# A decoder trunk on one core: the whole kernel in written order, native float32 scores of two heads in row halves, heads and accumulators in pairs

## The chip, the cores and the metric

The kernel runs on one core of a Trainium2 chip. The metric is the device time of the program in microseconds (us), as the median of three runs. PE is the tensor engine (TensorE), PEld its weight loads, DVE the vector engine, ACT the scalar engine, POOL the GpSimd engine and SP the sync engine, which here only issues DMAs. L12 is line 12 of the kernel.

## What is computed

One layer of a decoder for 256 tokens of 2048 values, in float32, with rms norms. `a` is the normed input:

```
in  = a @ W_in                      # 2048 x 2368: q and kv latents, rope key, window q, k, v
mla = 8 heads: softmax(causal((q_nope k_nope + q_rope k_rope) / sqrt(192))) v     # 256 x 256 each
swa = 16 heads of 64, 2 kv heads: softmax over the last 128 keys with a T5 bias and a sink
x  += [mla, swa] @ W_out            # 2048 x 2048
x  += relu(rms(x) @ W_up)**2 @ W_down   # 2048 x 8192, 8192 x 2048
out = rms(x)
```

The T5 bias of a head is a table of 32 values, looked up by a bucket of the distance of query and key (16 exact distances, then 16 logarithmic steps).

## The kernel before, in words

Every wide product is transposed: weights are the 128x128 stationary tile, the activation is the moving one, with 256 tokens as columns. Each weight block of 1024 columns is loaded by SP, rounded to a high part by ACT (L104, 1050 ns) and a low part by DVE (L105, 1253 ns); the activation holds a high and a low part as 512 columns. `mm_chunk` multiplies the high weight with all 512 columns (L114) and the low weight with the 256 high ones (L116). I call these two products **a pair**; 1024 weight columns are 8 pairs, and I call that **a step**. There are 64 pairs of the first four output tiles (k, v and two q tiles, L264 and L268), 240 of the other 15 tiles of the projection `in`, 32 of `kn`, a product for `v`, 48 of `qb`, 256 of `wo` and 2016 of `up` and `dn`, and the last two output tiles of `dn` in row halves (L764).

What stands between the pairs on PE:

- the T5 bias: sixteen tiles of 512 one-hot columns. Each is multiplied with the table's high and low part (L302, L303, 64 output rows), copied by ACT (L304) and written to DRAM by POOL's queue (L307); four loads bring it back in another layout (L314), and POOL masks the first half (L317).
- the window heads, two at a time (`t` = 0 to 7): scores `sa` and `sb` (L392, L396) of q and k split into high and low parts; DVE adds the bias (L403 to L407), maxima, ACT exponentials (L422) and the scaling by 1/sum (L428); four transposes (L435); the product with `v_sc`, which is padded with zeros so that two heads add up in one tile of 128 rows (L444, L448).
- the MLA heads, one at a time beside the first half of `wo`: `mla_scores` (L625 to L630), three transposes, `mla_pv`.
- the final norm: sums (L794), 32 transposes of the result (L804), a scaling of each group of four and a DMA of it, eight in all.

The order on each engine is set by the framework's scheduler from priorities and its own estimates, not by the order in which the code is written. PSUM is held in tiles of 512 columns: four for accumulators (`psd`), two for scores (`pss`), two for the rest (`pst`).

## Time and profile before

| what | us |
|---|---|
| median of three runs (lowest, highest) | 1032.0 (1028.16, 1032.9) |
| the profiled execution | 1032.6 |
| its span, first to last instruction | 1030.8 |
| PE busy | 1008.3 |
| DVE busy | 705.0 |
| ACT busy | 539.5 |

A row of a timeline gives the start, the length, the engine, the line, the operation, and output <- inputs with the shape. The length of a product is longer than the distance to the next one, since products are pipelined, so the distance of starts is what a product costs. A row marked x4 stands for four instructions; a native float32 product is recorded as two.

### The profile page before, as it was taken

Reading aid. Unit: us, or ns where it says so; the run is one execution under the profiler, and the core shown is the slowest. Engines: PE = TensorE matmul, PEld = TensorE weight load, DVE = VectorE, ACT = ScalarE, POOL = GpSimd, SP = SyncE. Lnnn points to the kernel's source line nnn. Section 1 sums busy time; section 2 is a strip of 40 time slices with the busy share of each in tenths; the row PEclk is TensorE's granted clock in tenths of the full one; section 3 lists DMA queues with packets and bytes.
Section 4 is the critical chain, followed back from the end, with each engine's and each line's share of the span. In section 5 each row is a group of like instructions: output and inputs, shape, how many; then the busy total and the mean of one; then the engine's idle time right before and its main releaser. Section 6 shows DMA issues by size and latency. Waiting matters only on the chain.

```text
span 1030.8 us, 15494 instructions
## 1 busy us (share of the span) xinstructions
PE 1008.3 (98%) x5854; PEld 886.8 (86%) x5854; DVE 705.0 (68%) x1123; ACT 539.5 (52%) x893; POOL 105.7 (10%) x112
## 2 busy tenths in 40 slices
PE   9989789999999999999999999999999999999997
PEld 8878678889888888888888888888888888888887
DVE  7895589798897866655566656566666556666664
ACT  6675599965664444333444433344443334445553
POOL 2121340551232200000000000000000000000000
PEclk9999899999999999999999999999999999999999
DMA  8957523353454655555555555555555555555552
GB/s 299 317 206 210 155 91 141 135 188 129 161 185 164 216 192 185 193 193 187 187 195 191 185 192 195 184 189 198 186 185 195 192 185 191 196 185 187 194 172 82
DMA packets 53450, 191.04 MB, mean 185 GB/s; under 512 B 6096, under 2 KB 6480, under 8 KB 52864
## 3 DMA queue, kind: packets, MB, share of 16 engines
q1 hardware_dynamic: 51840, 184.57, 51.1%
q0 software_dynamic: 1392, 5.41, 2.2%
q8 instruction: 46, 0.75, 0.3%
q14 instruction: 28, 0.23, 0.1%
q10 hardware_dynamic: 144, 0.07, 0.0%
HBM read 185.80 MB, written 4.23 MB: 184 GB/s over the span
## 4 chain that ended last, share of the span: by engine, by line
PE 85%; DMA 4%; DVE 4%; ACT 4%; issue 2%; POOL 0%; ACTq 0%; POOLq 0%; DVEq 0%
PE up L114 23%; PE dn L114 22%; PE up L116 12%; PE dn L116 11%; PE wo L114 5%; PE wo L116 3%; DMA raw_in<-in_w_in_dram 2%; DMA bias<-bias_scratch 2%; PE in L114 2%; DVE lo_in L105 1%; PE in L116 1%; PE dn L764 1%; PE yp L444 1%; ACT st L422 0%; DVE buck L243 0%
## 5 line engine op out<-in xcount | busy, mean ns | idle before, releaser
L114 PE MATMUL up<-ms,hi_up 128*128 128x512 f32 x1024 | 355.4, 392 | 0.0
L116 PE MATMUL up<-ms,lo_up 128*128 128x256 f32 x1024 | 287.7, 281 | 0.0
L104 ACT CAST hi_dn<-raw_dn 128x1024 fp32r<-128x1024 f32 x128 | 134.3, 1049 | 201.6 <-PE dn L114 161.2
L105 DVE TENSOR_TENSOR lo_up<-raw_up,hi_up 128x1024 fp32r<-128x1024 f32 x128 | 161.1, 1259 | 114.0 <-ACT hi_up L104 113.6
L114 PEld LDWEIGHTS up<-ms,hi_up 128*128 128x128 f32 x1024 | 192.1, 188 | 42.1
L104 ACT CAST hi_up<-raw_up 128x1024 fp32r<-128x1024 f32 x128 | 134.2, 1049 | 174.3 <-issue 133.6
L105 DVE TENSOR_TENSOR lo_dn<-raw_dn,hi_dn 128x1024 fp32r<-128x1024 f32 x128 | 156.9, 1226 | 96.1 <-ACT hi_dn L104 91.0
L116 PEld LDWEIGHTS up<-ms,lo_up 128*128 128x128 f32 x1024 | 192.5, 188 | 0.0
L114 PE MATMUL dn<-usB,hi_dn 128*128 128x512 f32 x496 | 174.9, 392 | 0.0
L114 PE MATMUL dn<-usC,hi_dn 128*128 128x512 f32 x496 | 174.9, 392 | 0.0
L116 PE MATMUL dn<-usB,lo_dn 128*128 128x256 f32 x496 | 139.4, 281 | 0.0
L116 PE MATMUL dn<-usC,lo_dn 128*128 128x256 f32 x496 | 139.4, 281 | 0.0
L114 PEld LDWEIGHTS dn<-usB,hi_dn 128*128 128x128 f32 x496 | 93.1, 188 | 20.4
L114 PEld LDWEIGHTS dn<-usC,hi_dn 128*128 128x128 f32 x496 | 93.1, 188 | 20.4
L116 PEld LDWEIGHTS dn<-usB,lo_dn 128*128 128x128 f32 x496 | 93.2, 188 | 0.0
L116 PEld LDWEIGHTS dn<-usC,lo_dn 128*128 128x128 f32 x496 | 93.2, 188 | 0.0
L114 PE MATMUL wo<-ys,hi_wo 128*128 128x512 f32 x256 | 90.5, 395 | 0.2 <-DVE mla L323 0.2
L114 PE MATMUL in<-xs,hi_in 128*128 128x512 f32 x240 | 86.9, 400 | 0.0
L116 PE MATMUL wo<-ys,lo_wo 128*128 128x256 f32 x256 | 72.4, 284 | 0.0
L116 PE MATMUL in<-xs,lo_in 128*128 128x256 f32 x240 | 68.8, 287 | 0.7 <-DVE lo_in L105 0.7
L105 DVE TENSOR_TENSOR lo_in<-raw_in,hi_in 128x1024 fp32r<-128x1024 f32 (+1 forms) x39 | 47.7, 1224 | 17.4 <-ACT hi_in L104 17.2
L114 PEld LDWEIGHTS wo<-ys,hi_wo 128*128 128x128 f32 x256 | 48.0, 188 | 10.4 <-DVE mla L323 0.5
(298 smaller groups left out, 1261.3 us busy)
## 6 DMA issues: line engine op xcount, KB each, us to landing
raw_up<-in_w_up_dram SPq DMA_DIRECT2D x128, 512.0 KB, 3.6
raw_dn<-in_w_down_dram SPq DMA_DIRECT2D x128, 512.0 KB, 3.6
raw_in<-in_w_in_dram SPq DMA_DIRECT2D x37, 512.0 KB, 6.0
raw_wo<-in_w_out_dram SPq DMA_DIRECT2D x32, 512.0 KB, 4.2
raw_qb<-in_w_q_b_dram SPq DMA_DIRECT2D x6, 512.0 KB, 3.7
xt<-in_x_tok_dram SPq DMA_DIRECT2D x2, 1024.0 KB, 8.1
bias_scratch<-biasT POOLq DMA_DIRECT2D x4, 512.0 KB, 5.3
bias<-bias_scratch POOLq DMA_DIRECT2D x4, 512.0 KB, 9.9
```

The source lines that it names most:

```text
L104: nc.scalar.copy(hi[:, :n], raw[:, :n])
L105: nc.vector.tensor_tensor(lo[:, :n], raw[:, :n], hi.bitcast(F32)[:, :n], op=ALU.subtract)
L114: nc.tensor.matmul(ps[:, 0:2 * S], lhsT=hi[:, col:col + P], rhs=act(k, 0, 2 * S), start=first, stop=False)
L116: nc.tensor.matmul(ps[:, S:2 * S], lhsT=lo[:, col:col + P], rhs=act(k, 0, S), start=False, stop=last)
L444: nc.tensor.matmul(yp[:, 0:S], lhsT=v_sc[:, 0, t // 4, j, :], rhs=pt[:, j, 0:2, :].rearrange("p i c -> p (i c)"), start=(j == 0), stop=False)
L764: nc.tensor.matmul(ps[:, b * S:(b + 1) * S].rearrange("p (a c) -> p a c", a=2), lhsT=hi[:, (k % 8) * P:(k % 8 + 1) * P], rhs=x[:, :, b, :] ...
```

## The change

The code is laid out as 332 steps of 8 pairs in a loop under `manual_schedule`, in which each engine keeps the order in which the code is written. Tables `pre`, `hook` and `post` name what is issued ahead of a step, before its k-th pair, and behind it; `w_hi` of a step is issued three steps ahead, `w_lo` two. The projection `in` takes steps 0 to 29, `kn` 30 to 33, `v` 34 to 37, `qb` 38 to 43, `wo` 44 to 75, then `up` and `dn`. Further:

- window scores: native float32 products of the unsplit q and k of 64 rows, one head in rows 0 to 63 and the other in rows 64 to 127 of the array (`swa_mm`: two products of 128 columns and two of 256); pair t at step 17+3t, its transposes at step 20+3t, its v product at 21+3t, where the two heads take the two column halves of the array instead of zero-padded values.
- T5 bias: the one-hot columns come from the distances themselves (ACT takes the absolute difference to an interval's middle, DVE compares), so the bucket loop on DVE is gone; four batches of four native float32 products of 512 columns, again in column halves; each batch is written to DRAM and loaded again by itself, and the mask comes at the end.
- MLA heads in pairs (`mla_mm`): native float32, 128 rows for the part without rope, row halves for the rope part.
- accumulators in pairs of 512 columns (`psd` two pairs, `pss` one), read by one instruction for two tiles.
- the roots for x, kv and q from a bit estimate and three Newton rounds on DVE instead of ACT's Sqrt; rope's turn by DMAs on POOL's queue; squares are added on DVE instead of POOL.
- the tail: 24 of the 32 final transposes, unscaled, stand in the last quarter of `dn` (`fin_turn`), four more ahead of the last row half; the result goes out in six DMAs on two queues.

PE, the projection, where the first bias tile stands. Before, `oh` is a one-hot tile, `rel_hi` and `rel_lo` the table, `in4` an output tile of the projection:

```order
L302 MATMUL bias0_0_679<-oh0_0_677,rel_hi_370 64x512
L303 MATMUL bias0_0_679<-oh0_0_677,rel_lo_371 64x512
L114 MATMUL in4_676<-xs_77,hi_in4_0_665 128x512
L116 MATMUL in4_676<-xs_77,lo_in4_0_666 128x256
...
L302 MATMUL bias0_1_693<-oh0_1_691,rel_hi_370 64x512
```

After, `g_sb` holds the table in float32, and `in1` is a pair of output tiles:

```order
L723 MATMUL in1_529<-xs_77,hi_6_488 128x512
L725 MATMUL in1_529<-xs_77,lo_6_527 128x256
L322 MATMUL bias0_561<-oh0_509,g_sb_78 64x512
L322 MATMUL bias0_561<-oh1_546,g_sb_78 64x512
L322 MATMUL bias0_561<-oh0_509,g_sb_78 64x512
L322 MATMUL bias0_561<-oh1_546,g_sb_78 64x512
L723 MATMUL in1_529<-xs_77,hi_6_488 128x512
```

Sixteen places with two products became four places with four, and they moved from the projection's fifth to eighth of the 15 tiles to steps 6 to 12, its fourth to seventh.

PE, the first window heads. Before, the scores stand between tiles 9 and 10 of the projection, and the transposes `tp0` of their softmax `st0` two tiles later:

```order
L116 MATMUL in9_1056<-xs_77,lo_in9_1_1052 128x256
L392 MATMUL sa0_1101<-kk_393,qs0_1096 128x256 x2
L396 MATMUL sb0_1102<-kk_393,qs0_1096 128x256 x4
L114 MATMUL in10_1144<-xs_77,hi_in10_0_1133 128x512
...
L114 MATMUL in12_1373<-xs_77,hi_in12_0_1362 128x512
L435 MATMUL tp0_1272<-ident_101,st0_1109 128x128 x2
L116 MATMUL in12_1373<-xs_77,lo_in12_0_1363 128x256
```

After, around the second pair of heads, `sw1` being its scores and `hi_20`, `lo_20` the weights of step 20:

```order
L723 MATMUL in5_1046<-xs_77,hi_20_943 128x512
L725 MATMUL in5_1046<-xs_77,lo_20_988 128x256
L417 MATMUL sw1_1049<-kd_371,q_s0_402 128x128 x2
L417 MATMUL sw1_1049<-kd_371,q_s0_402 128x256 x2
L723 MATMUL in5_1046<-xs_77,hi_20_943 128x512
...
L466 MATMUL tp0_1058<-ident_101,st0_972 128x128 x4
```

The transposes of one pair of heads now stand in the same step as the scores of the next, three steps behind their own scores.

DVE, the softmax of the first window heads. Before, `lo_in12_1` is the low part of a weight block, `bias` the loaded table:

```order
L403 TENSOR_TENSOR st0_1109<-sa0_1101,bias_392 128x2x128
L105 TENSOR_TENSOR lo_in12_0_1363<-raw_in12_0_1361,hi_in12_0_1362 128x1024
L404 TENSOR_TENSOR st0_1109<-sa0_1101,st0_1109 128x2x128
L403 TENSOR_TENSOR st1_1197<-sa1_1189,bias_392 128x2x128
L404 TENSOR_TENSOR st1_1197<-sa1_1189,st1_1197 128x2x128
L105 TENSOR_TENSOR lo_in12_1_1369<-raw_in12_1_1367,hi_in12_1_1368 128x1024
...
L407 TENSOR_TENSOR st0_1109<-st0_1109,bias_392 128x2x128
L407 TENSOR_TENSOR st1_1197<-st1_1197,bias_392 128x2x128
```

After:

```order
L1140 TENSOR_TENSOR lo_19_946<-raw_19_919,hi_19_920 128x1024
L426 COPY_PREDICATED st0_972<-mask_own_106,sw0_950 128x2x128
L429 SCALAR_TENSOR_TENSOR st0_972<-sw0_950,rx8_373,bias_369 128x2x128
L431 SCALAR_TENSOR_TENSOR st0_972<-st0_972,rx8_373,bias_369 128x2x128
L434 TENSOR_REDUCE nm0_977<-st0_972 128x4
L438 TENSOR_TENSOR nm0_977<-nm0_977,nsink_119 128x4
L440 TENSOR_TENSOR es0_980<-nm0_977,nsink_119 128x4
L1140 TENSOR_TENSOR lo_20_988<-raw_20_942,hi_20_943 128x1024
L1140 TENSOR_TENSOR lo_21_1016<-raw_21_984,hi_21_985 128x1024
L457 TENSOR_TENSOR l0_1006<-l0_1006,es0_980 128x4
```

Before, the softmaxes of two pairs of heads are interleaved with the weights of tile 12; after, each stands whole between the weights of steps 19 and 20, and the weights of steps 20 and 21 stand behind the instructions that read the bias.

The diff, cut to its core:

```diff
-    psd = ctx.enter_context(tc.tile_pool(name="psd", bufs=4, space=bass.MemoryType.PSUM))
-    pss = ctx.enter_context(tc.tile_pool(name="pss", bufs=2, space=bass.MemoryType.PSUM))
+    psd = ctx.enter_context(tc.tile_pool(name="psd", bufs=2, space=bass.MemoryType.PSUM))
+    pss = ctx.enter_context(tc.tile_pool(name="pss", bufs=1, space=bass.MemoryType.PSUM))
     pst = ctx.enter_context(tc.tile_pool(name="pst", bufs=2, space=bass.MemoryType.PSUM))
 
...
+    def dense_pair(name):
+        return psd.tile([P, 2, 512], F32, tag="d", name=name)
+
     def dense_ps(name):
-        return psd.tile([P, 512], F32, tag="d", name=name)
+        if not dense_half:
+            t = dense_pair(name)
+            dense_half.append(t[:, 1, :])
+            return t[:, 0, :]
+        return dense_half.pop()
 
     def score_ps(name):
-        return pss.tile([P, 512], F32, tag="s", name=name)
+        return pss.tile([P, 2, 512], F32, tag="s", name=name)
...
+    def newton(y, v, name, n, rounds):
+        t = small(f"nt_{name}", n)
+        for _ in range(rounds):
+            nc.vector.tensor_tensor(t, y, y, op=ALU.mult)
+            nc.vector.scalar_tensor_tensor(t, t, -0.5, v, op0=ALU.mult, op1=ALU.mult)
+            nc.vector.scalar_tensor_tensor(y, t, 1.5, y, op0=ALU.add, op1=ALU.mult)
+        return y
+
+    def rsqrt_bits(v, name):
+        y = small(f"y_{name}")
+        nc.vector.tensor_scalar(y.bitcast(I32), v.bitcast(I32), -0.5, 1597463007.0, op0=ALU.mult,
+                                op1=ALU.add)
+        return newton(y, v, name, 2, 3)
+
...
-    def bias_step(n):
-        b, e = divmod(n, 4)
-        o = b * 2048 + e * 512
-        oh = rot([P, 512], F32R, f"oh{b}_{e}")
-        nc.vector.tensor_scalar(oh, lanes[o // 4096][:, o % 4096:o % 4096 + 512],
-                                c_sb[:, 0:1], None, op0=ALU.is_equal)
-        ps = score_ps(f"bias{b}_{e}")
-        nc.tensor.matmul(ps[0:64, :], lhsT=rel_hi, rhs=oh, start=True, stop=False)
-        nc.tensor.matmul(ps[0:64, :], lhsT=rel_lo, rhs=oh, start=False, stop=True)
-        nc.scalar.copy(bias_box[0][:, b % 2, e * 4:e * 4 + 4, :],
-                       ps[0:64, :].rearrange("p (q c) -> p q c", c=P))
...
+    def oh_away(n):
+        oh = work.tile([P, 2, 512], F32, tag="oh", name=f"oh{n}", bufs=2)
+        o = n * 1024
+        nc.scalar.activation(oh.rearrange("p e c -> p (e c)"),
+                             lanes[o // 4096][:, o % 4096:o % 4096 + 1024], AF.Abs,
+                             bias=c_sb[:, 4:5])
+        oh_state[n] = oh
+
+    def oh_hot(n):
+        oh = oh_state[n]
+        nc.vector.tensor_scalar(oh, oh, c_sb[:, 5:6], None, op0=ALU.is_lt)
+
+    def bias_mm(n):
+        b, par = divmod(n, 2)
+        if par == 0:
+            bias_ps[b] = score_ps(f"bias{b}")
+            return
+        ps = bias_ps[b]
+        ohs = oh_state.pop(n - 1), oh_state.pop(n)
+        for e in range(2):
+            for p2, oh in enumerate(ohs):
+                nc.tensor.matmul(ps[p2 * 64:(p2 + 1) * 64, e, :], lhsT=rel_f, rhs=oh[:, e, :],
+                                 start=True, stop=True)
+
+    def bias_out(b):
+        nc.scalar.copy(biasT[:, b % 2, :, :], bias_ps.pop(b))
+        for p2 in range(2):
+            q0 = b * 16 + p2 * 8
             nc.gpsimd.dma_start(
-                scratch2[:, :, b * 16:(b + 1) * 16, :].rearrange("g h q c -> (g h) q c"),
-                bias_box[0][:, b % 2, :, :])
-
-    def bias_load():
-        for i in range(2):
-            for qh in range(2):
-                nc.gpsimd.dma_start(bias[qh * 64:(qh + 1) * 64, i, :, :],
-                                    scratch2[2 * i + qh].rearrange("h q c -> q h c"))
-            if i == 0:
-                nc.gpsimd.affine_select(out=bias[:, 0, :, :], in_=bias[:, 0, :, :],
-                                        pattern=[[0, NH_SWA], [-1, P]], compare_op=ALU.is_ge,
-                                        fill=NEG, base=0, channel_multiplier=1)
-
-    def sum_evac(dst, ps, name):
-        t = evac_sum(ps, name)
-        nc.vector.tensor_tensor(dst, ps[:, 0:S], t, op=ALU.add)
-
-    def scaled_evac(dst, ps, rstd, name):
-        t = evac_sum(ps, name)
-        nc.vector.tensor_tensor(t, ps[:, 0:S], t, op=ALU.add)
-        nc.vector.tensor_tensor(dst, t, rstd, op=ALU.mult)
+                scratch2[:, :, q0:q0 + 8, :].rearrange("g h q c -> (g h) q c"),
+                biasT[p2 * 64:(p2 + 1) * 64, b % 2, :, :].rearrange("p e (q c) -> p (e q) c", c=P))
+        for g in range(4):
+            q0 = (g % 2) * 64 + b * 16
+            nc.gpsimd.dma_start(bias[q0:q0 + 16, g // 2, :, :],
+                                scratch2[g, :, b * 16:(b + 1) * 16, :].rearrange("h q c -> q h c"))
+
+    def bias_mask():
+        nc.gpsimd.affine_select(out=bias[:, 0, :, :], in_=bias[:, 0, :, :],
+                                pattern=[[0, NH_SWA], [-1, P]], compare_op=ALU.is_ge,
+                                fill=NEG, base=0, channel_multiplier=1)
+
+    def pair_evac(dst, ps, name):
+        t = two(f"t_{name}", "evt2", 2)
+        nc.scalar.copy(t, ps[:, :, S:2 * S])
+        nc.vector.tensor_tensor(dst, ps[:, :, 0:S], t, op=ALU.add)
...
-        a = score_ps(f"sa{t}")
-        b = score_ps(f"sb{t}")
-        for j in range(2):
-            nc.tensor.matmul(a[:, j * S:(j + 1) * S].rearrange("p (w c) -> p w c", w=2),
-                             lhsT=qs[:, j, 0:P], rhs=kk[:, kv, :, 0:P], start=True, stop=True)
-        for j in range(2):
-            for w in range(2):
-                nc.tensor.matmul(b[:, j * S:(j + 1) * S], lhsT=qs[:, j, P:2 * P],
-                                 rhs=kk[:, kv, w, :], start=(w == 0), stop=(w == 1))
...
+    def swa_mm(t):
+        sc = score_ps(f"sw{t}")
+        for qs, cs, w in ((slice(0, P), slice(0, P), P), (slice(P, S), slice(P, P + S), S)):
+            for j, rows in enumerate((lo_h, hi_h)):
+                nc.tensor.matmul(sc[:, j, cs], lhsT=q_sb[t][rows, qs], rhs=kd[rows, t // 4, 0:w],
+                                 start=True, stop=True)
+        box[f"sc{t}"] = sc
+
+    def swa_max(t):
+        sc = box.pop(f"sc{t}")
         st = rot([P, 2, 2, P], F32, f"st{t}")
-        av = a.rearrange("p (j w c) -> p j w c", j=2, w=2)
-        bv = b.rearrange("p (j w c) -> p j w c", j=2, w=2)
         hs = slice(2 * t, 2 * t + 2)
-        nc.scalar.copy(st[:, :, 1, :], bv[:, :, 0, :])
-        nc.vector.tensor_tensor(st[:, :, 0, :], av[:, :, 1, :], bias[:, 0, hs, :], op=ALU.add)
-        nc.vector.tensor_tensor(st[:, :, 0, :], av[:, :, 0, :], st[:, :, 0, :], op=ALU.add)
+        nc.scalar.copy(st[:, :, 1, :], sc[:, :, P:2 * P])
...
+    def swa_pv(t):
+        pt, own = box.pop(f"pt{t}")
         yp = misc_ps(f"yp{t}")
+        kv = slice((t // 4) * 64, (t // 4) * 64 + 64)
         for j in range(2):
-            nc.tensor.matmul(yp[:, 0:S], lhsT=v_sc[:, 0, t // 4, j, :],
-                             rhs=pt[:, j, 0:2, :].rearrange("p i c -> p (i c)"),
-                             start=(j == 0), stop=False)
+            nc.tensor.matmul(yp[j * 64:(j + 1) * 64, 0:S], lhsT=vv[:, 0, kv],
+                             rhs=pt[:, j, :, :].rearrange("p i c -> p (i c)"),
+                             start=True, stop=False)
         for j in range(2):
-            nc.tensor.matmul(yp[:, P:S], lhsT=v_sc[:, 1, t // 4, j, :], rhs=pt[:, j, 2, :],
...
+    def turn_copy(key, src):
+        t = two(f"rt_{key}", "oh", 2)
+        n = src.shape[1]
         for o in range(0, P, 32):
-            nc.scalar.copy(t[o:o + 32, :], src[o ^ 32:(o ^ 32) + 32, :])
...
+    def mla_mm(p):
+        mla = box["mla"]
+        sc = score_ps(f"ms{p}")
+        for qs, cs, w in ((slice(0, P), slice(0, P), P), (slice(P, S), slice(P, P + S), S)):
+            for e in range(2):
+                nc.tensor.matmul(sc[:, e, cs], lhsT=mla[:, QN + 2 * p + e, qs],
+                                 rhs=mla[:, KN + 2 * p + e, 0:w], start=True, stop=False)
+            for e, rows in enumerate((lo_h, hi_h)):
+                nc.tensor.matmul(sc[:, e, cs], lhsT=mla[rows, QR + p, qs], rhs=krr[rows, 0:w],
+                                 start=False, stop=True)
+        box[f"ms{p}"] = sc
...
+    def fin_turn(g):
+        tp = score_ps(f"fo{g}")
+        for b in range(2):
+            for i in range(4):
+                nc.tensor.transpose(tp[:, b, i * P:(i + 1) * P], box["fin"][:, 0, b, 4 * g + i, :],
+                                    ident)
+        box[f"fo{g}"] = tp
+
+    def fin_copy(g):
+        tp = box.pop(f"fo{g}")
...
-            finish(b, g)
+        b = SW0 + 3 * t
+        pe(b, 1, swa_mm, t)
+        at(post, b, swa_max, t)
+        at(post, b + 1, swa_exp, t)
+        at(post, b + 2, swa_norm, t)
+        pe(b + 3, 3, swa_turn, t)
+        at(post, b + 3, swa_pt, t)
+        pe(b + 4, 5, swa_pv, t)
+        at(post, b + 4, y_out, NH_MLA + t)
...
+    def w_hi(n):
+        raw = wpool.tile([P, WH], F32, tag="raw", name=f"raw_{n}")
+        hi = wpool.tile([P, WH + 64], F32R, tag="whi", name=f"hi_{n}")[:, WOFF:WOFF + WH]
+        nc.sync.dma_start(raw, srcs[n])
+        nc.scalar.copy(hi, raw)
+        weights[n] = raw, hi
+
+    def w_lo(n):
+        raw, hi = weights[n]
+        lo = wpool.tile([P, WH + 64], F32R, tag="wlo", name=f"lo_{n}")[:, WOFF:WOFF + WH]
+        nc.vector.tensor_tensor(lo, raw, hi.bitcast(F32), op=ALU.subtract)
+        weights[n] = hi, lo
+
+    with tc.manual_schedule():
+        for n in range(3):
+            w_hi(n)
+        for n in range(2):
+            w_lo(n)
+        for s_ in range(NS):
+            for f in pre.get(s_, ()):
+                f()
+            if s_ + 3 < NS:
+                w_hi(s_ + 3)
+            if s_ + 2 < NS:
+                w_lo(s_ + 2)
+            if s_ < NS:
+                mms[s_](s_, weights.pop(s_))
...
```

## Rows read from the trace of the kernel before

**Rows 1.** The page: busy time; TensorE's granted clock in 40 slices.

```profile
PE 1008.3 (98%) x5854; PEld 886.8 (86%) x5854; DVE 705.0 (68%) x1123; ACT 539.5 (52%) x893; POOL 105.7 (10%) x112
PEclk9999899999999999999999999999999999999999
```

**Rows 2.** Timeline of PE (start us, length us, line, operation), middle of up.

```profile
500.11 0.39 PE L114 MATMUL up<-ms,hi_up 128*128 128x512 f32 x1
...
503.93 0.39 PE L114 MATMUL up<-ms,hi_up 128*128 128x512 f32 x1
```

**Rows 3.** Waits of PE, whole span: us in total, times, longest us.

```profile
PE tp L435 <- ACT st L428: 4.4, 1, 4.4
PE yp L444 <- DVE pt L440: 3.1, 4, 1.4
PE sb L396 <- DVE st L404: 2.4, 1, 2.4
PE vps L365 <- DVE vT L350: 1.5, 1, 1.5
```

**Rows 4.** Timeline of PE, 112 to 130 us: the first window heads.

```profile
113.01 0.40 PE L392 MATMUL sa<-kk,qs 128*128 128x256 f32 x2
...
113.72 0.40 PE L114 MATMUL in<-xs,hi_in 128*128 128x512 f32 x1
...
120.90 0.77 PE L435 MATMUL tp<-ident,st 128*128 128x128 f32 x2 [4.35 <-ACT st L428]
...
123.39 0.63 PE L114 MATMUL in<-xs,hi_in 128*128 128x512 f32 x1
...
126.59 0.40 PE L114 MATMUL in<-xs,hi_in 128*128 128x512 f32 x1
...
127.18 1.02 PE L444 MATMUL yp<-pt,v_sc 128*128 128x256 f32 x4
128.04 0.61 PE L448 MATMUL yp<-pt,v_sc 128*128 128x128 f32 x4
128.49 0.50 PE L195 MATMUL ts_kv<-ones,acc_kv 128*128 128x1 f32 x4
```

**Rows 5.** Timeline of PE, one bias tile and the pair behind it.

```profile
55.05 0.39 PE L302 MATMUL bias<-oh,rel_hi 128*64 128x512 f32 x1
55.28 0.39 PE L303 MATMUL bias<-oh,rel_lo 128*64 128x512 f32 x1
55.51 0.39 PE L114 MATMUL in<-xs,hi_in 128*128 128x512 f32 x1
```

**Rows 6.** Timeline of PE: `wo` begins; the scores of one MLA head.

```profile
202.11 0.50 PE L114 MATMUL wo<-ys,hi_wo 128*128 128x512 f32 x1 [0.18 <-DVE mla L323]
...
205.00 0.28 PE L625 MATMUL ms<-qk 128*128 128x256 f32 x1
...
205.95 0.40 PE L114 MATMUL wo<-ys,hi_wo 128*128 128x512 f32 x1
```

**Rows 7.** Timeline of POOL: the last bias write, the mask behind the loads.

```profile
86.48 0.54 POOL L307 DMA_DIRECT2D bias_scratch<-biasT  x1 [6.88 <-ACT biasT L304]
...
102.86 2.01 POOL L317 TENSOR_SCALAR_AFFINE_SELECT bias<-bias 128x2048 f32<-128x2048 f32 x1 [7.85 <-DMA bias<-bias_scratch]
```

**Rows 8.** DVE, groups by line and form (busy us, mean ns): weights' low parts.

```profile
L105 DVE TENSOR_TENSOR lo_in<-raw_in,hi_in 128x1024 fp32r<-128x1024 f32 x37 | 46.4, 1253 | 16.5 <-ACT hi_in L104 16.3
```

**Rows 9.** Timeline of DVE, two instructions one behind the other.

```profile
124.06 0.42 DVE L328 TENSOR_TENSOR c_q<-t_q,rstd_x 128x256 f32<-128x256 f32 x1
124.39 0.42 DVE L440 TENSOR_TENSOR pt<-tp,mask_ownT 128x256 f32<-128x256 f32 x1
```

**Rows 10.** Timeline of PE and ACT, the tail.

```profile
1019.07 1.11 PE L764 MATMUL dn<-usC,hi_dn 128*128 128x256 f32 x8
...
1020.38 1.29 PE L804 MATMUL fo<-ident,fin 128*128 128x128 f32 x10
...
1024.60 0.69 ACT L809 ACTIVATE fin<-fo,y_f 128x512 f32<-128x512 f32 x1 [0.17 <-PE fo L804]
```

More of the change, by code (lines that the diff above doesn't have):

```diff
@@ L352 @@
[L352 to L362 removed]
+    rx8 = small("rx8")
@@ L378 @@
[L378 to L397 removed]
+        box["vps"] = vps
@@ new lines, in c_add, with c_sums, c_mean @@
+    def c_add(which):
+        a, b = acc_c[which, 0], acc_c[which, 1]
+        nc.vector.tensor_tensor(a, a, b, op=ALU.add)
+    def c_sums(which):
+        ps = misc_ps(f"ts_{which}")
+        a = acc_c[which, 0]
+        for b in range(2):
+            for i in range(2):
+                nc.tensor.matmul(ps[:, b:b + 1], lhsT=a[:, i, b * P:(b + 1) * P],
+                                 rhs=ones[:, 0:1], start=(i == 0), stop=(i == 1))
+        box[f"ts_{which}"] = ps
+    def c_mean(which):
+        v = small(f"ms_{which}")
+        nc.vector.scalar_tensor_tensor(v, box.pop(f"ts_{which}")[:, 0:2], 1.0 / LORA, epsx,
+                                       op0=ALU.mult, op1=ALU.add)
+        box[f"v_{which}"] = v
```

1056 lines of the change are left out of this document (627 added, 429 removed).

## The prediction

> **What bounds the kernel now.** I read the page first. PE is busy for 1008.3 us of the span, 98% [rows 1], so only two things can move the time: what stands on PE, and the few microseconds in which PE waits. In the middle of `up` eleven pairs start within 3.82 us [rows 2], .347 us for a pair and 2.78 for a step of eight. The number of pairs isn't changed, so from `wo` on, where PE runs at this pace, the change can win nothing but can lose. The list of PE's waits shows where it stands still: 4.4 us at the first window transposes, 3.1 at the window value products, 2.4 for a score buffer, 1.5 for the transposes of v, 11.4 in all [rows 3], all ahead of `wo`, which starts at 202.11 [rows 6]. The timeline then shows what such a wait leaves behind: after the 4.35 us stop at 120.90 a wide product lasts .63 instead of .40, and the pace of .40 is back at 126.59 [rows 4]; in the page's row of granted clocks the fifth slice is the only low one of the stretch [rows 1]. Between these times stand seven pairs and four transposes, 7 x .347 + 4 x .113 = 2.9 us at full pace, done in 5.7: 2.8 lost. Last, the length of a product is .39 and the distance to the next start .23 [rows 5]; the difference, .16, comes into the open once after every stop. PE stopped seven times in those four rows: 1.1.
>
> **What goes.** The transposes of a pair of heads stand three steps (8.3 us) behind its scores, with nothing of another pair's softmax ahead of them; before, two softmaxes were interleaved, and the last scaling came 4.4 us too late. The value products stand a step behind the transposes, the score buffer is asked for again after three steps, the transposes of v come long after v. If DVE and ACT keep up, all four waits go, with their restarts and the slow clock: 11.4 + 1.1 + 2.8 = 15.3 us. The waits not shown stay in the sum as an allowance for small new ones.
>
> Whether DVE keeps up: in steps 17 to 42 it has 26 weight blocks of 1.25 us [rows 8], 33 us, eight softmaxes of about ten instructions, 35, and some seventy instructions of evacuations and norms, about .4 each as in [rows 9], 28. That is 96 beside some 92 us of PE work. But an instruction of .42 us is followed by the next after .33 [rows 9], which makes it about 76. I take no wait from this, and keep 4 us (96 - 92) as the upper bound.
>
> **What is put in other forms.** Native float32 costs, from 127.18 to 128.49: two products of 256 columns .86, two of 128 columns .45, so .43 and .225 each, in two records each [rows 4]. Now, for each group, (1) what it costs before; (2) if the two halves of the array run one after the other; (3) if the second record of one half runs beside the first of the other half, since PE takes its instructions in order and neighbours alone can share; (4) if halves run fully side by side.
>
> Bias: before 16 x .46 (55.05 to 55.51, [rows 5]) = 7.4. After, four batches of four products of 512 columns, .86 each: (2) 13.8, (3) five records of .43 instead of eight, 8.6, (4) 6.9.
> Window scores: before 8 x .71 (113.01 to 113.72, [rows 4]) = 5.7. After, two products of .225 and two of .43: (2) 8 x 1.31 = 10.5, (3) 8 x .87 = 7.0, (4) 5.2.
> Window values: before 8 x 1.31 = 10.5; after (2) 10.5, (3) 7.0, (4) 5.2.
> MLA scores: before 8 x .95 (205.00 to 205.95, [rows 6]) = 7.6. After, a pair of heads has 1.31 of full-height products and 1.31 in halves: (2) 10.5, (3) 9.2, (4) 7.9.
> Together against before: (2) +14.1, (3) +.8, (4) -6.0. No row shows two halves of the array at work, so the price lies between (2) and (4). I take (3), which asks only that two neighbours on different rows or columns don't wait for each other. Eight more products of one column (`c_sums`; two took .50 at most, [rows 4]) add up to 2; I take 1.
>
> The Trainium skill ("TensorE: Matmul & The Clock Gate", Part 3 on packing small matmuls) says that products at different tile positions run concurrently in the array; no row here shows it, and by it the sum would come to price (3) or (4).
>
> **The tail.** 28 of the 32 last transposes now stand ahead of the last product instead of behind it. Ten take 1.29 us, less the open .16 .113 each [rows 10]: +3.2 on PE before the last product ends. Behind it, before, the last product ends at 1020.18, the last scaling at 1025.29, and the span at 1030.8. After, there are still two additions, a square, sums, the root, a scaling of 768 columns and one of 512, and DMAs. The root hides no longer behind transposes, but the scaling waited for the last transposes, not for the root, by .17 [rows 10]. I take no change, bounds -1 and +1.5.
>
> **What is hidden.** The bucket loop, the split of q and k, the additions on POOL and the bit-estimate roots are work beside PE. The bit roots add six short DVE instructions each and take an ACT step away; two or more steps lie between the sums and the product that spreads the root, so I cost them at nothing; without that cover each would cost some 1 us. The rope turn goes to POOL's queue, which has nothing queued behind it there.
>
> **The sum.** -15.3 + .8 + 1.0 + 3.2 = -10.3. The profiled execution took 1032.6, .6 over the median of 1032.0; from the median I come to 1021.7, and say 1021.5. The case's own range goes from 1012 (price (4), and the small waits gone too) to 1026 (DVE's 4 us).
>
> **Rivals.**
> *Halves one after the other.* Price (2): 13.3 more, 1035. For it: nothing in the trace runs side by side on PE. Against it: nothing in it could. The change would then be lost in what it pays on PE.
>
> *The bias comes late.* DVE's L429 reads the masked bias in step 17, and `lo_20` and `lo_21` are queued behind it on DVE. Before, 18.4 us passed from the issue of the last write (86.48) to the end of the mask (104.87), 7.85 of it waiting for loads [rows 7]. After, the last batch is copied at the start of step 13, and DVE comes to L429 about 12 us later. If the way takes 18.4 again, DVE stands for 6.4; PE, two steps (5.6) ahead less 3.8 of softmax and weight work, stops for 4.6, and pays a slow clock again, 2.8: 1029. Against it: only a quarter of the table is still under way then, so I'd put the mask 0 to 6 us early.
>
> *Drains, the slower side.* PE now goes from full tiles to half tiles and back: 16 times for window scores, 16 for values, 8 for the bias, 16 for MLA, 56 in all. If PE must empty at each, the open .16 [rows 5] is paid 56 times, +9. With price (2) that is 1044, slower; with price (3) 1030.5. From price (2), .04 us a switch are enough for slower. Against it: the bias tiles of before are 64 columns wide and stand among full ones, and 55.05, 55.28 and 55.51 lie .23 apart, with no gap on the way out of the narrow tile [rows 5]. Row halves have no such row, and a weight load that can't be hidden would make a switch dearer still.
>
> The Trainium skill ("TensorEngine Tiling (Array Packing)", Key Properties) states that changing the tiling mode drains TensorE, which speaks against this change; the row at 55.51 shows no drain for narrow tiles, and no run shows row halves.
>
> **Chances.** Halves shared, bias in time (1021.5): .54. Bias late (1029): .13, of which I give .04 to a lateness so small that the result is still faster. One after the other (1035): .12. Drains with shared halves (1030.5): .07. Drains with halves one after the other (1044): .14. What a measurement of this kernel can tell from no change is about 0.5%, 5.2 us: faster below 1026.8, slower above 1037.2. So faster .54 + .04 = .58, same .09 + .12 + .07 = .28, slower .14. The range from 1011 to 1036 holds all but the last case and about .04 at the ends of the first.
>
> **What would show it.** In the profile after: `wo` starts at about 187 if all is right (202.1 less 15.3; bias +1.2, scores +1.3, values -3.5 and the sums +1.0 cancel), at about 199 with price (2). From the first score product of a pair of window heads to the next wide one .87 says price (3), 1.31 price (2), .66 price (4); for a batch of bias 2.15, 3.44, 1.72. A start more than .23 behind that of the last half tile says drain. The list of waits has no row of over 1 us in the projection, and the slices of the granted clock show no 8 in the fifth; a wait of `lo_20` for L429, and of that for POOL's mask, says late bias. From the end of the last row-half product to the end of the span it is 10.6 (1030.8 less 1020.18, [rows 10]) as before. I'm wrong if PE waits in steps 17 to 42 as often as before, in smaller pieces, for low parts of weights: then DVE is the bound there, or if the steps of `up` are longer than 2.78.

## The result and the profile after

The changed kernel takes 1036.7 us (median of nine runs, 1035.0 to 1040.0) against 1030.8 of the kernel before in the same measurement (nine runs, 1028.2 to 1032.9): ratio 1.0059, 95% interval 1.0043 to 1.0076. It is slower by .6%; I had forecast 1021.5 and faster.

PE's waits of the changed kernel (us in total, times, longest) stand beside those of [rows 3]:

```profile
PE in L725 <- DVE lo L1140: 6.5, 1, 6.5
PE tp L466 <- DVE st L460: 1.8, 2, 1.4
PE in_kv L272 <- ACT hi_in L113: 1.5, 1, 1.5
PE bc_x L370 <- DVE dg_x L364: 1.4, 1, 1.4
PE ts_q L517 <- DVE sq_q L510: 1.2, 1, 1.2
```

Of the four waits of [rows 3] three are gone, as forecast, and the window transposes wait 1.8 in place of 4.4. But one of 6.5 stands in their place. It can be followed upward, from PE's timeline to DVE's and POOL's. First PE, columns as in [rows 4]:

```profile
98.80 0.40 PE L723 MATMUL in<-xs,hi 128*128 128x512 f32 x1
105.67 0.58 PE L725 MATMUL in<-xs,lo 128*128 128x256 f32 x1 [6.48 <-DVE lo L1140]
...
111.35 0.63 PE L723 MATMUL in<-xs,hi 128*128 128x512 f32 x1
```

PE has the high part of step 20's weights, but not the low part. DVE, which makes it:

```profile
91.23 0.45 DVE L426 COPY_PREDICATED st<-mask_own,sw 128x256 f32<-128x256 int32 x1 [0.81 <-ACT st L425]
102.49 0.48 DVE L429 SCALAR_TENSOR_TENSOR st<-sw,rx,bias 128x256 f32<-128x256 f32 x1 [10.81 <-POOL bias L338]
...
104.40 2.35 DVE L1140 TENSOR_TENSOR lo<-raw,hi 128x1024 fp32r<-128x1024 f32 x2
```

DVE stands for 10.81 us for the masked bias, and the two low parts are behind it. POOL, which writes, loads and masks the bias, to be held against [rows 7]:

```profile
77.50 1.09 POOL L329 DMA_DIRECT2D bias_scratch<-biasT  x2
85.10 2.29 POOL L334 DMA_DIRECT2D bias<-bias_scratch  x4 [6.51 <-DMA bias_scratch<-biasT]
87.37 1.09 POOL L329 DMA_DIRECT2D bias_scratch<-biasT  x2
95.96 2.28 POOL L334 DMA_DIRECT2D bias<-bias_scratch  x4 [7.50 <-DMA bias_scratch<-biasT]
100.45 2.00 POOL L338 TENSOR_SCALAR_AFFINE_SELECT bias<-bias 128x2048 f32<-128x2048 f32 x1 [2.21 <-DMA bias<-bias_scratch]
```

Each group of four loads waits on the queue until the write before it has landed, and the next write stands behind these loads. So the last write is issued at 87.4, where I had put it at the start of step 13 (about 76), and the mask ends at 102.5. That is the late bias, my second case, in a dearer form. After the stop PE's products again take .63 instead of .40 until 112; from 105.7 on that is 6.4 us at half the clock (granted .50 in this stretch), some 3 of them lost.

By stages, from marks in the two timelines:

| stage | before | after | difference | forecast |
|---|---|---|---|---|
| start to the projection's fifth tile | 30.4 | 31.3 | +.9 | 0 |
| from there to `wo` (202.1, 201.4) | 171.7 | 170.1 | -1.6 | -15.3 |
| `wo` (to 308.1, 309.3) | 106.0 | 107.9 | +1.9 | +1.6 |
| `up`, `dn`, last row halves (to 1020.2, 1024.3) | 712.1 | 715.0 | +2.9 | +3.2 |
| tail (to 1030.8, 1034.0) | 10.6 | 9.7 | -.9 | 0 |

The second line misses by 13.7 us, as much as the whole (+3.2 measured, -10.5 forecast; by its own prices the prediction's other forms add up to +.6, not the +.8 of its sum, hence -10.5 and not -10.3). The transposes that were moved cost 2.9 in the fourth line and give .9 back in the last. The first line's .9 is within what this mark moves by: in the other runs of the changed kernel it comes at 30.1 to 32.7.

### The profile page after: what moved, and what is told of

It is laid out like the page before. It is cut to its first block, busy times and chain, and to the rows that moved or that the text cites. A ratio compares the mean times of both kernels' runs of the same rounds, so it can differ in the third digit from the quotient of the medians.

```text
span 1034.0 us, 14909 instructions
## 1 busy us (share of the span) xinstructions
PE 1011.6 (98%) x5878; PEld 877.0 (85%) x5878; DVE 648.1 (63%) x870; ACT 508.9 (49%) x719; POOL 30.6 (3%) x63
## 4 chain that ended last, share of the span: by engine, by line
PE 89%; DMA 4%; DVE 3%; ACT 1%; issue 1%; POOL 1%; SPq 0%; DVEq 0%; ACTq 0%; POOLq 0%
PE up L723 23%; PE dn L723 22%; PE up L725 12%; PE dn L725 11%; PE wo L723 6%; PE wo L725 3%; PE in L723 3%; DMA bias_scratch<-biasT 3%; PE in L725 1%; PE qb L723 1%; PE last L1044 1%; DVE lo L1140 1%; DMA raw_in<-in_w_in_dram 1%; POOL bias L334 1%; PE in_kv L272 1%
## 5 line engine op out<-in xcount | busy, mean ns | idle before, releaser
L1134 ACT CAST hi<-raw 128x1024 fp32r<-128x1024 f32 x332 | 348.3, 1049 | 330.5 <-PE dn L723 179.5
L1140 DVE TENSOR_TENSOR lo<-raw,hi 128x1024 fp32r<-128x1024 f32 x332 | 398.9, 1220 | 65.4 <-ACT hi L1134 64.0
L723 PE MATMUL up<-ms,hi 128*128 128x512 f32 x1024 | 355.4, 392 | 0.0
L723 PE MATMUL dn<-us,hi 128*128 128x512 f32 x992 | 344.5, 392 | 0.0
L725 PE MATMUL up<-ms,lo 128*128 128x256 f32 x1024 | 287.7, 281 | 0.0
L725 PE MATMUL dn<-us,lo 128*128 128x256 f32 x992 | 278.8, 281 | 0.0
L723 PEld LDWEIGHTS up<-ms,hi 128*128 128x128 f32 x1024 | 192.2, 188 | 42.1
L723 PEld LDWEIGHTS dn<-us,hi 128*128 128x128 f32 x992 | 186.1, 188 | 40.8
L725 PEld LDWEIGHTS up<-ms,lo 128*128 128x128 f32 x1024 | 192.5, 188 | 0.0
L725 PEld LDWEIGHTS dn<-us,lo 128*128 128x128 f32 x992 | 186.5, 188 | 0.0
L723 PEld LDWEIGHTS wo<-ys,hi 128*128 128x128 f32 x256 | 48.1, 188 | 11.3 <-issue 1.3
```

Source lines behind the costliest of these rows:

```text
L723: nc.tensor.matmul(ps[:, 0:2 * S], lhsT=hi[:, col:col + P], rhs=act(k, 0, 2 * S), start=first, stop=False)
L725: nc.tensor.matmul(ps[:, S:2 * S], lhsT=lo[:, col:col + P], rhs=act(k, 0, S), start=False, stop=last)
L1134: nc.scalar.copy(hi, raw)
L1140: nc.vector.tensor_tensor(lo, raw, hi.bitcast(F32), op=ALU.subtract)
```

## The experiments

Three theories stood at first: the order on POOL's queue makes the bias late (Q); DVE is the bound in the window stretch (D); the transfers themselves are slow, whatever their order (L).

**e1_queue.** The loads of a batch go behind the write of the next one:

```diff
+        if b > 0:
+            bias_in(b - 1)
+        if b == 3:
+            bias_in(3)
+
+    def bias_in(b):
         for g in range(4):
```

> The changed kernel with one edit on POOL's queue: the loads of bias batch b are issued behind the write of batch b+1, so no write stands behind loads that wait for the write before it. Theory Q (POOL's queue makes the bias late): in the changed kernel a batch took about 10 us of queue (writes issued at 56.2, 65.1, 77.5, 87.4), though its batches are ready every 7.6 us; here the last write is issued at about 76, the mask ends at about 91 instead of 102.5, L429 waits for under 1 us instead of 10.8, PE's stop of 6.5 us and the 6.4 us at half clock (about 3 lost) are gone: 9 to 10 us faster than the changed kernel, about 1027, ratio to the kernel before about .996. Theory D (DVE is the bound in the window stretch): the stop only breaks into smaller ones, 3 us or less gained. Theory L (the DMAs themselves are slow, not their order): the mask still ends after 98.

Measured: 1033.6 (before 1031.2), ratio 1.0024 (1.0010 to 1.0038), so some 3 us better than the changed kernel. POOL and DVE of this run:

```profile
78.41 1.09 POOL L329 DMA_DIRECT2D bias_scratch<-biasT  x2 [3.81 <-ACT biasT L326]
...
87.45 2.23 POOL L340 DMA_DIRECT2D bias<-bias_scratch  x4 [4.30 <-DMA bias_scratch<-biasT]
97.77 2.01 POOL L344 TENSOR_SCALAR_AFFINE_SELECT bias<-bias 128x2048 f32<-128x2048 f32 x1 [8.09 <-DMA bias<-bias_scratch]
```

```profile
99.81 0.48 DVE L435 SCALAR_TENSOR_TENSOR st<-sw,rx,bias 128x256 f32<-128x256 f32 x1 [4.85 <-POOL bias L344]
```

The last write is issued nine us earlier, as Q says, but it lands nine us after its issue, and the loads behind it take ten. DVE still waits 4.85 for the mask, and PE's stop is 4.4. Nine of the us won on the queue became three: Q is a part of the miss, and what is left is the long way itself, as L says.

**e2_sw18.** `SW0` = 18 instead of 17.

> The changed kernel with the first window heads at step 18 instead of 17, and all later ones a step later; POOL's queue as it is. Theory Q: the mask still ends at about 102.5, L429 stands one step (2.8 us) later and waits 8 instead of 10.8, and PE's stop is 3 to 4 us instead of 6.5. Theory D: the stop stays near 6.5, since DVE's load moves along.

Measured: one time, 1039.5; PE's stop is 6.8. Both theories seem to fail, but the mask ended at 106.2 in this run, not 102.5: its last loads were issued at 97.4 after a wait of 9.0 for the write. The landing times differ by microseconds from run to run, so a step more of distance says little.

**e3_nobias** and **e10_before_nobias.** In the changed kernel, and later in the kernel before, the writes and loads of the bias are left out and the table is zeros:

```diff
-        for p2 in range(2):
-            q0 = b * 16 + p2 * 8
-            nc.gpsimd.dma_start(
...
+        if b == 0:
+            nc.gpsimd.memset(bias, 0.0)
```

> The changed kernel without the bias's way through DRAM: writes and loads are left out and the table is filled with zeros, so the window heads' bias is left out of the computation. Nothing is ever late for the bias then. Theory Q: as the run with the reordered queue, 1026 to 1027, and no more than 1 us better than it. Theory D: PE still stops between 95 and 110 for several us in all. Were bias DMAs also a burden for the weights' DMAs, this run would be faster than the reordered one by more than 1 us.

> The kernel before without the bias's way through DRAM, the table filled with zeros, so the window heads' bias is left out of the computation. It tells what that way costs the kernel before, where PE waited 2.4 and 4.4 us about it and lost 2.8 at half clock. If these waits are the bias's: 1031.3 - 9 = about 1022, and the rest of the change (e3_nobias 1026.7) would be a loss of 4 to 5 us by itself. If they came from the order of the softmax work: 1028 to 1031, and the rest of the change a gain of 2 to 4.

Measured: 1026.7 for the changed kernel, and 1024.3 for the kernel before, one time each. PE's waits of the changed kernel without bias traffic:

```profile
PE tp L459 <- DVE st L453: 1.8, 2, 1.4
PE in_kv L276 <- DVE lo_in L114: 1.3, 1, 1.3
PE ts_q L510 <- DVE sq_q L503: 1.2, 1, 1.2
```

and in the kernel before without it, where the wait of 4.4 in [rows 3] has shrunk to .3, that of 3.1 to .7, and that of 2.4 no longer stands in the list; that of 1.5 for the transposes of v stays:

```profile
PE bias L302 <- DVE oh L299: 2.9, 2, 2.5
...
PE vps L359 <- DVE vT L344: 1.4, 1, 1.4
...
PE yp L438 <- DVE pt L434: 0.7, 1, 0.7
...
PE tp L429 <- ACT st L422: 0.3, 1, 0.3
```

This is the main result. The stop at the window transposes, which I had put down to the order of the softmax work, was the bias's in the kernel before too. By the marks of the table above, one execution each, without bias traffic in the last two columns:

| stage | before | after | before (e10) | after (e3) |
|---|---|---|---|---|
| start to the projection's fifth tile | 30.4 | 31.3 | 31.8 | 31.9 |
| from there to `wo` | 171.7 | 170.1 | 162.5 | 160.0 |
| `wo` | 106.0 | 107.9 | 105.5 | 107.9 |
| `up`, `dn`, last row halves | 712.1 | 715.0 | 712.1 | 715.0 |
| tail | 10.6 | 9.7 | 10.7 | 9.9 |

So the bias's way costs the stretch ahead of `wo` 9 us in the kernel before and 10 in the changed one. Without it the change wins 2.6 there and loses 4.5 from `wo` on, and the changed kernel is the slower by some 2. From `wo` on the stages agree within .2 in all runs of the changed kernel that leave them alone (kernel before and e10: within .5), so this loss is not noise. D has fallen as the cause of the stop: in e3_nobias no low part of a weight makes PE wait in the window stretch. What DVE does cost is smaller: the waits of 1.4 (the longest of `tp`) and 1.2 (`ts_q`) stay without bias traffic, and DVE's rows show it at work without a gap for 9 us ahead of the first and 2.6 ahead of the second.

The DMA queues between 70 and 100 us show what the way does to others; first the changed kernel, then e3_nobias (queue: packets, MB, share of the 16 engines; then issues with the median time to landing):

```profile
q1 hardware_dynamic: 1403, 5.09, 48.1%
q0 software_dynamic: 1026, 3.08, 43.6%
...
raw<-in_w_in_dram SPq DMA_DIRECT2D x7, 512.0 KB, 6.2
bias<-bias_scratch POOLq DMA_DIRECT2D x12, 128.0 KB, 5.4
bias_scratch<-biasT POOLq DMA_DIRECT2D x4, 256.0 KB, 7.0
```

```profile
q1 hardware_dynamic: 1586, 5.77, 56.2%
...
raw<-in_w_in_dram SPq DMA_DIRECT2D x10, 512.0 KB, 4.5
```

The weights, with x, alone take over half of the engines' time (56.2%), the bias and its way back take most of the rest, and a weight block lands in 6.2 us instead of 4.5. So there is a fourth theory, B: the bias's traffic fills the engines and delays the weights and itself.

**e6_early.** e1_queue with the bias's work two steps earlier (`BIAS0` = 1).

> The reordered queue of e1_queue, and the bias's work two steps earlier (one-hot columns from step 1 instead of 3). In e1_queue the last write was issued at 78.4, landed at 87.5, the loads took until 97.8, and L429's place was 95. Theory Q+L (the way through DRAM is long, 19 us for the last batch, and started too late): the mask ends about two steps earlier, at 92 to 94, ahead of L429's place; PE's stop of 4.4 and the half clock go, and the time is that of the run without bias traffic, 1026 to 1028, ratio .995 to .997. Theory B (the bias traffic holds back the weights themselves): PE stops elsewhere between 60 and 100, and the time stays over 1030.

Measured: 1034.0, ratio 1.0030 (1.0017 to 1.0042). The stop for `lo` is nearly gone, but another one is there:

```profile
PE bc_x L376 <- DVE dg_x L370: 5.2, 1, 5.2
...
PE in L731 <- DVE lo L1146: 1.3, 2, 0.8
```

ACT's rows tell from where: it now waits for the weights and for x's pieces themselves.

```profile
72.45 1.06 ACT L365 ACTIVATE xt<-xt 128x1024 f32<-128x1024 f32 x1 [2.44 <-DMA xt<-in_x_tok_dram]
...
76.08 1.05 ACT L1140 CAST hi<-raw 128x1024 fp32r<-128x1024 f32 x1 [2.48 <-DMA raw<-in_w_in_dram]
```

B holds: x's pieces, like the weights, come late, and the stop moves to the product that waits for x's sum of squares.

**e4_order** and **e7_half.** Two runs on the halves of the array. e4 swaps the two loops of `swa_mm`, so that both products of the lower rows come first; e7 lets both heads use the lower rows:

```diff
-  nc.tensor.matmul(sc[:, j, cs], lhsT=q_sb[t][rows, qs], rhs=kd[rows, t // 4, 0:w],
+  nc.tensor.matmul(sc[:, j, cs], lhsT=q_sb[t][lo_h, qs], rhs=kd[lo_h, t // 4, 0:w],
```

> The changed kernel with the four score products of a pair of window heads in another order: both of the lower rows, then both of the upper rows. Theory N (only neighbours on different halves share time, each product being two records): of the eight records one shares its time instead of three, so the body of a pair takes .1125 x 2 + .215 + .215 + .1125 + .43 = 1.20 us instead of .85. Theory F (halves run freely side by side, whatever the order): it stays at .85 or goes to .66. Theory S (halves never share, and .85 has another reason): it stays at .85. The time of the whole grows by 8 x .35 = 2.8 us by N.

> The changed kernel, but the score products of both heads of a pair use rows 0 to 63 (so the second head's scores are those of the first: it is left out of the computation). No two products of a pair can then lie on different halves. Theory F (halves run side by side, in any order, and .2 us are fill and drain): the body of a pair goes from .86 to about 1.31 + .2 = 1.5. Theory H (nothing is shared; a product of 64 rows is simply cheaper than one of 128): the body stays at .86.

The times are 1036.8 for e4 and 1040.9 for e7, one each. PE around a pair's scores, in the changed kernel and then in e7_half:

```profile
120.43 0.27 PE L725 MATMUL in<-xs,lo 128*128 128x256 f32 x1
120.64 0.93 PE L417 MATMUL sw<-kd,q_s 64*128 64x128 f32 x8
121.49 0.50 PE L723 MATMUL in<-xs,hi 128*128 128x512 f32 x1
121.83 0.28 PE L725 MATMUL in<-xs,lo 128*128 128x256 f32 x1
```

```profile
122.24 1.57 PE L417 MATMUL sw<-kd,q_s 64*128 64x128 f32 x8
123.75 0.50 PE L723 MATMUL in<-xs,hi 128*128 128x512 f32 x1
```

The body is .85 with both halves, 1.51 with one, and .86 in e4, whatever the order. By [rows 4] the products of one half take 1.31 one after the other and .655 when two halves share fully; .2 is added in both cases. So the halves run side by side, not only neighbours, and N of e4 falls, as do S and H. What is paid for it besides stands at the edges: the product ahead of a group of half tiles is followed .09 later than usual (120.43 to 120.64, .21 instead of .116), and the wide product behind it by .34 instead of .23, .11 more. But only the first is a price of half tiles: behind native groups of full tiles, too, the wide product is followed .31 to .33 later (122.65 to 122.96 behind four transposes; 53.58 to 53.90 in the kernel before), and ahead of them nothing is lost (213.05 to 213.17). The price of 1.06 in all is .19 above what I had taken, .87, and made up otherwise. (The Trainium skill, "TensorE: Matmul & The Clock Gate", Part 3, has products at different tile positions run concurrently; .85 against 1.51 agrees. The Trainium skill, "TensorEngine Tiling (Array Packing)", Key Properties, has a change of tiling mode drain the engine; the .09 ahead of row halves agrees, and the bias's column halves show the same .09 ahead of a body of 1.87, though the narrow tiles of [rows 5] had shown none.)

**e5_mla_tail.** MLA: all full-height products of a pair, then all of 64 rows (two changes of tile size fewer). Tail: `send(0, y0)` ahead of the last `hi_pass`.

> The changed kernel with two independent edits. MLA scores: all four full-height products of a pair first, then all four of 64 rows, so two changes of tile size fewer for each pair. If each change costs about .1 as at the other places, the body goes from 2.65 to about 2.4; if the price is that of products one after the other (2.62 by the rows of before) with no cost of changes, it stays at 2.65. Tail: the scaling and sending of the first 128 rows is written ahead of the last row half's products, not behind them; the last root no longer waits for it on DVE, and the end of the span lies .7 to 1.0 nearer to the end of the last product (9.8 in the changed kernel).

One time of 1035.3. The scores of a pair of MLA heads, first in the changed kernel, then here:

```profile
202.44 0.61 PE L611 MATMUL ms<-mla 128*128 128x128 f32 x4
202.97 0.49 PE L614 MATMUL ms<-krr,mla 64*128 64x128 f32 x4
203.39 1.13 PE L611 MATMUL ms<-mla 128*128 128x256 f32 x4
204.46 0.70 PE L614 MATMUL ms<-krr,mla 64*128 64x256 f32 x4
205.09 0.50 PE L723 MATMUL wo<-ys,hi 128*128 128x512 f32 x1
```

```profile
204.03 1.47 PE L611 MATMUL ms<-mla 128*128 128x128 f32 x8
205.44 0.93 PE L615 MATMUL ms<-krr,mla 64*128 64x128 f32 x8
206.29 0.50 PE L724 MATMUL wo<-ys,hi 128*128 128x512 f32 x1
```

2.65 becomes 2.26: .39 for two switches between native groups (out of and into the half tile), about .2 each on average, and 1.6 us for the four pairs (`wo` takes 106.3 here instead of 107.9). The tail is 9.2 instead of 9.7 behind the last product.

**e8_sum, e9_sum2, e11_later, e12_xearly.** What these runs point to, put together: e1_queue, `SW0` = 18, both edits of e5, and three instructions of PE moved a little later (x's spread, `c_sums`, the window transposes).

> What the runs point to, in one kernel: the changed kernel with POOL's queue reordered (as e1_queue), the window heads one step later (step 18), the MLA order and the tail of e5_mla_tail, and three places moved within a step or by one: the product that spreads x's root half a step later, c_sums four pairs later, the window transposes three pairs later. By parts from the changed kernel's 1036.7: stop and half clock 6.5 + 3 gone (e1_queue still had a stop of 4.4, a step later it is about 1.6 or none), waits of 1.4, 1.2 and 1.8 gone, MLA -1.6, tail -.5: 1036.7 - 9.5 + 1.6 - 4.4 - 2.1 = 1022, ratio .992. Theory B (the bias traffic holds back weights and the x pieces): some of the waits come again at other places, 1024 to 1028.

> The same with the bias's work a step earlier (one-hot columns from step 2). If the bias's end decides, the last stop of e8_sum goes too: 1 to 2 us better. If its traffic decides, it meets the x pieces and the weights earlier, as in e6_early, and the product that spreads x's root waits: the same or 1 to 3 us worse.

> e8_sum with the window heads another step later (steps 19, 22, 25, 28, 31, 34, 37 and 39 instead of 18 to 39 by threes), the last pair packed two steps behind the one before. In e8_sum the mask ended at 99.6, 3.3 us of PE's waits hung on it, with a half clock behind. If only the bias's end is late, these go: 1024 to 1026, ratio .993 to .995. If the weights are what the bias's traffic delays, PE's wait for a low part of weights stays at 2 to 3 us. Packing the last heads may cost a wait at the last transposes of about 1.

> e8_sum with the four x pieces (512 KB each, for the sum of squares) loaded in steps 1 to 4 instead of 4, 6, 8 and 10, ahead of nearly all bias traffic. In e8_sum the 16 DMA engines are busy all the time from 70 to 100 us. If that is what makes weights and bias late, 1.5 MB less there (about 8 us of the traffic of that stretch at 190 GB/s) bring the mask 3 us or more forward, and the stop of 3.3 goes: 1024 to 1026. If the four pieces only make the first weights late, PE waits between 30 and 50 instead, and the time stays at 1028 to 1030.

| run | median | before, same chip | ratio (95%) | largest waits of PE |
|---|---|---|---|---|
| e8_sum | 1029.0 | 1032.3 | .9976 (.9963 to .9989) | `lo` 3.3, `tp` 1.3 |
| e9_sum2 | 1027.9 | 1032.3 | .9973 (.9959 to .9988) | `lo` 2.6, `bc_x` 1.6 |
| e11_later | 1032.7 | 1030.7 | 1.0023 (1.0009 to 1.0037) | `lo` 3.4, `qb` 2.6, `kn` 2.2 |
| e12_xearly | 1033.2 | 1030.7 | 1.0026 (1.0011 to 1.0040) | `lo` 7.8, `in_kv` 1.6 |

The first two are faster than both kernels, by a quarter of a per cent of the kernel before and .8% of the changed one. They are less good than expected. I had put the 3.3 of e8_sum down to the mask, which ends at 99.6. Its rows, ACT's and then DVE's, say otherwise: ACT's rounding waits for a weight block, ACT's copy of the scores stands behind it, and DVE comes to the bias a microsecond after the mask and doesn't wait for it:

```profile
98.93 1.05 ACT L1141 CAST hi<-raw 128x1024 fp32r<-128x1024 f32 x1 [2.90 <-DMA raw<-in_w_in_dram]
...
100.28 0.44 DVE L432 COPY_PREDICATED st<-mask_own,sw 128x256 f32<-128x256 int32 x1 [3.52 <-ACT st L431]
100.62 0.48 DVE L435 SCALAR_TENSOR_TENSOR st<-sw,rx,bias 128x256 f32<-128x256 f32 x1
```

So it is the late weights that are left, and the other two runs agree: with more distance (e11) PE still waits 3.4 for low parts, and packing the last heads brings larger waits at `qb` and `kn`; with x's pieces early (e12) PE stops for 4.3 at 52, the bias starts 6 us later, DVE waits 3.9 for the mask again, and the stretch is as full as before. DMA share and GB/s between 70 and 100 in e3_nobias, the changed kernel and e8_sum, the last two columns:

```profile
70.00:100.00 30.00, 30.00 (x177) 24.37 (x176) 21.08 (x44) 20.30 (x33) 0.00 (x0) 1.00 0.57 193
```

```profile
70.00:100.00 30.00, 27.60 (x157) 22.11 (x155) 14.47 (x31) 15.65 (x20) 9.00 (x16) 1.00 0.92 274
```

```profile
70.00:100.00 30.00, 29.23 (x167) 23.55 (x166) 14.67 (x31) 12.31 (x18) 11.05 (x17) 1.00 1.03 258
```

**e13_packets.** e8_sum with loads of 8 KB pieces, so that heads and queries change places:

```diff
-    scratch2[g, :, b * 16:(b + 1) * 16, :].rearrange("h q c -> q h c"))
+    scratch2[g, :, b * 16:(b + 1) * 16, :])
```

> e8_sum with the same bytes of bias over the same queue at the same places, but each load reads 8 KB in a piece for each partition instead of sixteen pieces of 512 bytes; heads and queries of the table are thereby exchanged, so the window heads' bias is another one than the reference's. Theory P (the small pieces cost the DMA engines their time): between 70 and 100 us the DMA engines are busy for .6 to .8 instead of 1.03, weights land in about 5 us instead of 9.2, the mask ends 5 us or more earlier, PE's waits for weights go, and the time is near that of the run without bias traffic plus the edits of e8_sum, about 1024. Theory Y (the bytes, or the way DRAM to DRAM by itself): share, landing times and the stop stay as in e8_sum, 1028 to 1030.

One time, 1026.5 (before 1030.2; e8_sum took 1027.6 to 1030.5). The share is 1.02, weights land in 8.9 us between 60 and 100 (9.2 in e8_sum), bias loads in 8.3 (9.5), the stop is 2.6 (3.3). So the small pieces are not the cause, or a small part. In the changed kernel 3.1 MB of bias in 30 us take 43.6% of the engines' time beside 48.1% for 5.1 MB of weights and x, so a byte of the bias costs half as much again as one of the weights (43.6/3.08 against 48.1/5.09). The trace of e13 tells the bias's writes and loads apart, since their packets differ in size: between 70 and 100 us a write's packet of 4 KB took 160 ns on average (1.05 MB in 8.5% of the engines' time), a load's of 8 KB 613 ns (1.79 MB in 28.0%), and one of 4 KB of the weights 242. The loads are the dear half. Why they are was not tried; that each fills only 16 partitions, where a weight block fills 128, is one difference that no run changed.

## Why the prediction was wrong

*What goes* is the step that failed. I took the four waits of [rows 3] for a matter of the order of softmax instructions, since the list named ACT and DVE as releasers, and removed them with their slow clock, 15.3 us. In the kernel before, three of them hung on the bias: e10 takes its traffic away and leaves .3 of 4.4, .7 of 3.1 and nothing of 2.4, with the old order; the 1.5 for the transposes of v stays at 1.4. With the traffic gone on both sides, the change wins 2.6 us ahead of `wo`, not 15.3. That the bias stood behind the waits was to be seen one releaser further up, in DVE's timeline of the kernel before:

```profile
115.33 0.76 DVE L407 TENSOR_TENSOR st<-st,bias 128x256 f32<-128x256 f32 x2 [4.30 <-DMA bias<-bias_scratch]
```

The last load of the bias, issued behind the mask of [rows 7], ends DVE's wait at 115.3; maxima, exponentials and scaling follow, and the transposes stop waiting at 120.9. With the change DVE comes to the bias at 91.7, where it came to it at 101.3 before, 9.6 us earlier, and the last write is issued at 87.4, .9 later than before. So the waits went and came back as one of 6.5, with others of 1.8, 1.4 and 1.2: in the window stretch PE's waits add up to 11.6 us instead of 14.3, and the clock gives nothing back. That, with the dearer forms below, is what is left of -15.3: -1.6.

*The bias comes late* had the right place, instruction and followers, with .13, and was sized too low: 7.4 us (4.6 and 2.8 of clock), where the stop measured 6.5 and the clock some 3, and the other new waits 4.4 (1.4 of these goes with the bias's traffic in e3, 3.0 stay). Two terms of it were wrong. The last write was put at the start of step 13; it was issued 11 us later, 9 of them because it stood on the queue behind the wait of the loads before it (78.4 in e1_queue). And I took the way itself to be shorter than before, since only a quarter of the table was still under way; but the queue spreads the same bytes beside the same weights, and a batch takes 15 us from write to mask (87.4 to 102.5), against 18.4 for the whole.

*Prices in other forms.* By the edges of each group in the timeline, with both switches: bias 4 x 2.07 = 8.3 (forecast 8.6), window scores 8 x 1.06 = 8.5 (7.0), values 8 x 1.00 = 8.0 (7.0), MLA 4 x 2.76 = 11.0 (9.2): together +4.6 against the 31.2 before, where my own prices gave +.6 (the +.8 of the sum was a slip). The mechanism was wrong in detail: halves share fully (price 4; shown for row halves by e7, for column halves only by their sums), and the rival of drains was partly right, at .09 ahead of each group of half tiles. The error is 4 us by these groups. Not all of it reaches the time: MLA's scores cost 3.4 more, but `wo` takes only 1.9 more, .6 of the difference being waits of the kernel before; the rest was not followed.

*c_sums*: +1.0 forecast, .91 + .81 against .36 + .36 measured, right. *Transposes ahead of the last product*: +3.2 forecast, 24 in 2.37 and four in .39 plus .3 for edges, right. *Tail*: no change forecast, -.9 measured, within the bounds. *DVE*: nothing taken for its load, 4 us as the bound; it doesn't hold back weights, but the waits of 1.8 (`tp`) and 1.2 (`ts_q`) are its own, 3.0 in all, inside the bound. *Bit-estimate roots at nothing*: the spread of x's root made PE wait 1.4, with nine instructions of the three rounds in front of it on DVE, 1.7 us. But e3 has the same rounds and no such wait, so this one too hangs on the bias's traffic, and the roots' cover was enough without it.

The range ended at 1036, and 1036.7 is just outside; from 1030.8, the median of nine, instead of the 1032.0 from which I started, the miss is a microsecond larger.

## What to carry to other kernels

A wait is named by its last releaser. Before it is put down as removable, the chain above the releaser has to be followed, across engines, to something that the change moves; a run that takes the suspected source away in the kernel before settles it (here 4.4 became .3).

A table that goes to DRAM and back beside a stream of weights costs twice: its own lateness, and that of the weights. Moving its parts in time (e6, e12) shifted the stop to another tile here, with the engines' share in that stretch at about 1.

Where transfers that depend on each other share an in-order queue, write them so that no producer stands behind the wait of an earlier consumer.

## What the runs showed of the hardware

Two row halves of the array work fully side by side on native float32, in whatever order their products are written (.85 or .86 against 1.51 us for a pair of heads on one half). A group of half tiles costs .09 on the way in; the .11 behind it is paid, but for some .02, behind native groups of full tiles as well. Between native groups two changes of tile size cost .39.

A packet of the bias's loads from DRAM took 613 ns for 8 KB where one of its writes took 160 for 4 KB (e13_packets), in a stretch in which the engines' share was 1.02.

The landing times of the same transfers move by microseconds between executions of nearly the same program: the last group of bias loads waited 7.5, 9.0 and 11.3 us for its write in three runs with the same queue, which is why one step of distance could not be measured.

A stop of PE of 6.5 us was followed by 6.4 us at half the clock, one of 4.4 us in the kernel before by 5.7; a stop of 3.3 in e8_sum likewise by a low stretch (granted .83 on average between 100 and 110). In e10, without such a stop, no slice of the window stretch is low.
